# The edges of a feed-forward stage re-ordered: where stores, sums, squares, plain products and the last gains are issued

## The chip, the cores and the metric

One core of one Trainium2 chip runs one encoder layer in float32. The metric is the device time of one execution in microseconds (us), as the median of several runs. Engine names: PE is TensorE, DVE is VectorE, ACT is ScalarE, POOL is GpSimd, SP is SyncE, which issues most DMAs.

## What is computed

512 positions of width 2048 pass through a mixer (state-space and attention heads, not touched here), the output projection `w_out`, a feed-forward stage of width 5632 and an embedding gate:

```python
x = x + concat([y_ssd, y_mla]) @ w_out
h = rms_norm(x, ffn_norm_w)
u = causal_dwconv(h @ w_ffn_up, ffn_conv_w, ffn_conv_b)   # width 3
gate, up = u[..., :D_FF], u[..., D_FF:]
x = x + (silu(gate) * up) @ w_ffn_down
g = sigmoid(rms_norm(x, ple_norm_w) @ w_ple_gate + b_ple_gate)
x = x + g * rms_norm(p @ w_ple_proj, ple_post_norm_w)
return rms_norm(x, final_norm_w)
```

## The kernel before

**Products.** Every float32 operand is split into a high and a low part, and a product takes three matmuls (`acc3`: hi*hi, hi*lo, lo*hi). In the feed-forward both parts are float16: `Scaled.two` has ACT write the high part of a weight unit (`w`, L1040) and DVE the low part (L1041), after a scale `scq` is known for the group of units.

**Units and steps.** A weight unit is 512 x 256 values (512 KB). The up product has 11 chunks `c`, each of four groups `gi` of four units; the down product has groups of two units. `work` lists their order: from chunk 1 on, each up group is followed by a down group of an earlier chunk. One call of `Scaled.step` belongs to one unit: it writes out the parts of the unit two ahead (`split(i + 3)`), the load of the unit nine ahead (`load(i + 10)`, on SP), the look at the unit eight ahead (`look(i + 9)`: ACT takes the sum of absolute values of `raw` into `wst`, L997), POOL's block sums (`sums`), and whatever stands in the tables `first` and `agenda` for this step. Then the unit's matmuls are written out, and in their middle `mid` puts a tiny matmul `tot` (L250) for a group whose looks are complete (`stat`, L266); DVE makes the scale from it (L258 to L260).

**Plain and block units.** A plain unit (`plain_mm`) has 24 matmuls of 512 columns. A block unit (`blocks_mm`, L1242) forms each 2 x 2 block product with seven multiplications, 42 matmuls of 256 columns; it needs POOL's sums of the weight and of the activations, and DVE puts its four PSUM banks together in `blocks_out` (L1264 to L1268), where a plain group has two banks and no such step. In chunk 0 the first `PLAIN` groups are plain. There are seven banks for products. The activations `z` become float16 pairs `x0`, `x1` in `prep_a` (all 512 columns), POOL overwrites `z` with sums in `prep_sums`, `prep_b` makes `x3` and `x2` of them, and `prep_c` overwrites the upper half of `x0`, which plain units read as it was.

**The order of the work.** From the line `feed.enter_context(tc.manual_schedule())` to the end of the feed-forward, each engine's instructions stand in the order in which the code writes them. An engine takes its own queue strictly in order. Ahead of chunk 0 stands a prologue: the embedding projection (`proj.mm`, 16 PSUM banks `pp`, each copied by ACT to `prj` and stored to DRAM as `pnd`), mixed with `prep_a`. The feed-forward's banks are opened when `psum` is closed (`php.close()`).

**Later.** From chunk 1's end on, each of 17 steps runs one entry of `spare`: `proj_square` loads a `prj` tile back into one of three buffers `f` and has ACT sum its squares (L926); `proj_norm` follows. In the last eight down units, `renorm` makes the pair `xg` of each finished `xT[j]` (ACT `xgh`, DVE `xgl`) and adds its square to the sum `n2`, right behind the DVE instruction that finishes `xT[j]` (L1390).

## Time and profile before

| what | value |
|---|---|
| median of 3 runs | 2255.2 us (2254.92 to 2260.88) |
| the profiled execution: its time, its span | 2259.95 us, 2257.9 us |
| mean granted TensorE clock in it | 0.98 |
| PE, DVE, ACT, POOL busy | 96%, 68%, 58%, 43% of the span |

The profile shows one execution; its span runs from the first to the last instruction. PE's busy share is an upper bound: matmuls overlap, and one that runs at half clock counts as busy for twice the time. Slices in which fewer matmuls start than elsewhere are therefore read beside it.

### The profile page before, as it was taken

Reading aid. Unit: us, or ns where it says so; the run is one execution under the profiler, and the core shown is the slowest. Engines: PE = TensorE matmul, PEld = TensorE weight load, DVE = VectorE, ACT = ScalarE, POOL = GpSimd, SP = SyncE. Lnnn points to the kernel's source line nnn. Section 1 sums busy time; section 2 is a strip of 40 time slices with the busy share of each in tenths; the row PEclk is TensorE's granted clock in tenths of the full one; section 3 lists DMA queues with packets and bytes.
Section 4 is the critical chain, followed back from the end, with each engine's and each line's share of the span. In section 5 each row is a group of like instructions: output and inputs, shape, how many; then the busy total and the mean of one; then the engine's idle time right before and its main releaser. Section 6 shows DMA issues by size and latency. Waiting matters only on the chain.

```text
span 2257.9 us, 34811 instructions
## 1 busy us (share of the span) xinstructions
PE 2166.0 (96%) x13476; PEld 1618.2 (72%) x13476; DVE 1536.6 (68%) x2364; ACT 1315.5 (58%) x2031; POOL 961.1 (43%) x949
## 2 busy tenths in 40 slices
PE   9999999999997889879999999999999999999998
PEld 7888887777884377546777777777777777755886
DVE  5597767666437677455778777777777777765545
ACT  4333434433335767566777777777777777755324
POOL 3203320000125465435666566566666666613111
PEclk9999998999998989989999999999999999999999
DMA  7432222322224223333333333333333333333432
GB/s 244 140 99 84 67 60 71 98 71 93 95 92 140 93 94 95 121 102 114 113 113 107 109 103 113 108 109 113 111 114 104 113 112 113 103 102 141 145 108 84
DMA packets 211877, 243.27 MB, mean 108 GB/s; under 512 B 8192, under 2 KB 187520, under 8 KB 211328
## 3 DMA queue, kind: packets, MB, share of 16 engines
q1 hardware_dynamic: 210144, 236.53, 32.9%
q0 software_dynamic: 1280, 4.20, 0.5%
q8 instruction: 105, 1.72, 0.3%
q14 instruction: 60, 0.49, 0.1%
q10 hardware_dynamic: 288, 0.34, 0.0%
HBM read 228.45 MB, written 12.58 MB: 107 GB/s over the span
## 4 chain that ended last, share of the span: by engine, by line
PE 69%; DVE 12%; DMA 7%; ACT 7%; issue 2%; POOL 2%; SPq 0%; ACTq 0%; DVEq 0%; POOLq 0%
PE pu L1242 21%; DVE w L1041 5%; PE pn L160 4%; PE pn L162 4%; PE pn L161 4%; PE pd L160 3%; PE pd L161 3%; PE pd L162 3%; DMA raw<-in_w_ffn_up_dram 3%; PE pw L160 3%; DMA prj<-pnd 3%; PE pw L161 3%; PE pw L162 3%; PE pg L162 2%; PE pg L161 2%
## 5 line engine op out<-in xcount | busy, mean ns | idle before, releaser
L1242 PE MATMUL pu<-x,w 128*128 128x256 f16 x6888 | 767.1, 274 | 14.3 <-DVE e L1264 7.2
L1242 PEld LDWEIGHTS <-w 128*128 128x128 f16 x6888 | 673.2, 98 | 105.6 <-DVE e L1264 7.8
L1041 DVE SCALAR_TENSOR_TENSOR w<-raw,scq,w 128x768 f16<-128x768 f32 (+1 forms) x264 | 339.7, 1287 | 242.6 <-ACT w L1040 240.6
L997 ACT ACTIVATE junk<-raw 128x1024 fp8e4<-128x1024 f32 x264 | 277.6, 1052 | 241.2 <-DMA raw<-in_w_ffn_down_dram 123.3
L1040 ACT ACTIVATE w<-raw,scq 128x768 f16<-128x768 f32 (+1 forms) x264 | 266.1, 1008 | 80.3 <-PE pn L162 47.6
L160 PE MATMUL pn<-h,w 128*128 128x512 f16 x704 | 270.4, 384 | 12.7 <-DVE e L1264 8.7
L162 PE MATMUL pn<-h,w 128*128 128x512 f16 x704 | 270.0, 384 | 4.3 <-DVE w L1041 4.3
L161 PE MATMUL pn<-h,w 128*128 128x512 f16 x704 | 270.4, 384 | 0.0
L1027 POOL TENSOR_TENSOR sum<-raw 128x256 f32<-128x256 f32 x164 | 147.1, 897 | 250.2 <-DVE sct L258 137.8
L137 ACT CAST whi<-raw 128x1024 fp32r<-128x1024 f32 x108 | 113.0, 1049 | 226.4 <-PE pg L162 75.6
L138 DVE TENSOR_TENSOR wlo<-raw,whi 128x1024 fp32r<-128x1024 f32 x108 | 140.6, 1302 | 146.7 <-ACT whi L137 142.1
L1041 DVE SCALAR_TENSOR_TENSOR w<-sum,scq,w 128x1024 f16<-128x1024 f32 x164 | 233.5, 1424 | 5.2 <-ACT w L1040 2.3
L1340 POOL TENSOR_TENSOR o<-o,e 128x510 f32<-128x510 f32 x82 | 114.7, 1409 | 219.9 <-ACT e L1335 219.9
L1040 ACT ACTIVATE w<-sum,scq 128x1024 f16<-128x1024 f32 x164 | 186.1, 1135 | 2.5 <-PE pu L1242 2.1
L160 PEld LDWEIGHTS <-w 128*128 128x128 f16 x800 | 79.0, 99 | 129.6 <-issue 27.4
L1030 POOL TENSOR_TENSOR sum<-raw,sum 128x256 f32<-128x256 f32 x164 | 169.1, 1031 | 0.0
L1029 POOL TENSOR_TENSOR sum<-raw 128x256 f32<-128x256 f32 x164 | 157.0, 957 | 0.0
L162 PEld LDWEIGHTS <-w 128*128 128x128 f16 x800 | 79.2, 99 | 108.5 <-DVE w L1041 8.9
L161 PEld LDWEIGHTS <-w 128*128 128x128 f16 x800 | 79.0, 99 | 98.5 <-issue 16.9
L198 POOL TENSOR_TENSOR n1sq<-n1sq,n1sq 128x512 f32<-128x512 f32 x14 | 20.7, 1480 | 272.7 <-ACT n1sq L192 272.7
L1028 POOL TENSOR_TENSOR sum<-sum,raw 128x256 f32<-128x256 f32 x164 | 129.1, 787 | 12.9
L1390 DVE SCALAR_TENSOR_TENSOR xT<-pn,inv,xT 128x512 f32<-128x512 f32 x176 | 124.3, 744 | 4.3 <-PE pn L162 0.9
(368 smaller groups left out, 3927.1 us busy)
## 6 DMA issues: line engine op xcount, KB each, us to landing
raw<-in_w_ffn_up_dram SPq DMA_DIRECT2D x176, 512.0 KB, 3.5
raw<-in_w_ffn_down_dram SPq DMA_DIRECT2D x88, 512.0 KB, 3.5
raw<-in_w_in_dram SPq DMA_DIRECT2D x40, 512.0 KB, 3.6
raw<-in_w_out_dram SPq DMA_DIRECT2D x32, 512.0 KB, 3.5
raw<-in_w_ple_gate_dram SPq DMA_DIRECT2D x32, 512.0 KB, 3.7
raw<-in_w_in_dram SPq DMA_DIRECT2D x16, 424.0 KB, 3.9
xd<-xt POOLq DMA_DIRECT2D x16, 256.0 KB, 4.5
xT<-xd SPq DMA_DIRECT2D x16, 256.0 KB, 3.8
```

Of the source, the lines that this page charges most:

```text
L138: nc.vector.tensor_tensor(lo, raw, hi.bitcast(F32), ALU.subtract)
L160: nc.tensor.matmul(ps, a[0], b[0], start=first, stop=False)
L161: nc.tensor.matmul(ps, a[0], b[1], start=False, stop=False)
L162: nc.tensor.matmul(ps, a[1], b[0], start=False, stop=last)
L997: nc.scalar.activation(junk, self.raw[i], AF.Abs, accum_out=st[0][:, st[1]:st[1] + 1], saturate=False)
L1027: e(t[:, 0], r[:, :, 0], r[:, :, 2], ALU.add)
L1028: e(t[:, 1], t[:, 0], r[:, :, 1], ALU.subtract)
L1029: e(t[:, 2], r[:, :, 1], r[:, :, 0], ALU.subtract)
L1030: e(t[:, 3], r[:, :, 3], t[:, 1], ALU.subtract)
L1040: nc.scalar.activation(v[0], src, AF.Copy, scale=q)
L1041: nc.vector.scalar_tensor_tensor(v[1], src, q, v[0], ALU.mult, ALU.subtract)
L1242: nc.tensor.matmul(ps, wt[wi], xx[xi], start=st0 and i == 0 and half == 0, stop=sp0 and i == 2, skip_group_check=True)
```

## The change

Six edits, the diff cut to its core:

1. The 16 stores of `pnd` are issued by POOL instead of SP.
2. The looks at units 4 to 8 leave the prologue; those at 4 to 7 stand in step 0 between the last `prep_a`, and `early` passes their `stat` on within step 1.
3. `prep_sums` for all pairs is written in step 2, the last pair first (it was two pairs a step from step 2); `prep_b` moves from steps 5 to 8 to steps 8 to 11, and `prep_c` from steps 11 to 14 to steps 15 to 18.
4. `PLAIN` goes from 3 to 4, so that all of chunk 0 is plain.
5. The `out` of the first block group, (c, gi) = (1, 0), stands in `first`, ahead of the step's weight split.
6. A square's load and its sum stand two steps apart, one pair for each up group from chunk 2 on; `gain_hi` (with the square) and `gain_lo` stand one and two steps behind the unit that finishes `xT[j]`.

```diff
-                nc.sync.dma_start(pnd[t, nb], pr)
+                nc.gpsimd.dma_start(pnd[t, nb], pr)
...
-    def proj_square(t, nb, new):
-        pr = new("prj")
-        nc.sync.dma_start(pr, pnd[t, nb])
-        nc.scalar.activation(junk[:, :512], pr, AF.Square, accum_out=pss[:, t, nb:nb + 1], saturate=False)
+    pload = {}
+    def proj_load(t, nb, new):
+        pload[t, nb] = new("prj")
+        nc.sync.dma_start(pload[t, nb], pnd[t, nb])
+    def proj_square(t, nb):
+        nc.scalar.activation(junk[:, :512], pload[t, nb], AF.Square, accum_out=pss[:, t, nb:nb + 1], saturate=False)
...
-    def renorm(j, gname, nsum):
-        xg[j] = split_gain(xT[j], C(gname, j, j + 1), "xg")
-        nsum.add(xT[j])
+    def gain_hi(j):
+        xg[j] = slot("xgh", F32R), slot("xgl", F32R)
+        nc.scalar.activation(xg[j][0], xT[j], AF.Copy, scale=C("pleg", j, j + 1))
+        n2.add(xT[j])
+    def gain_lo(j):
+        nc.vector.scalar_tensor_tensor(xg[j][1], xT[j], C("pleg", j, j + 1), xg[j][0].bitcast(F32),
+                                       ALU.mult, ALU.subtract)
...
+        def early(self):
+            self.st16old.update(self.st16)
+            self.st16 = {}
...
-            self.look(i + 9)
+            if i:
+                self.look(i + 9)
...
-    PLAIN = 3
+    PLAIN = 4
...
-    fw.look(5)
     for t in range(NT):
         proj.mm(3, t)
-        fw.look(6 + t)
...
-                    for k in (0, 1):
-                        if 2 <= n < 6:
-                            plan(agenda, 1, lambda kp=n * 2 - 4 + k: prep_sums(kp))
-                        if 5 <= n < 9:
-                            plan(agenda, 1, lambda kp=n * 2 - 10 + k: prep_b(kp))
-                        if PLAIN * 4 - 1 <= n < PLAIN * 4 + 3:
-                            plan(agenda, 1, lambda kp=(n - PLAIN * 4 + 1) * 2 + k: prep_c(kp))
-                    if n < 2:
-                        for j in range(8 + n * 4, 12 + n * 4):
+                    if n == 2:
+                        for kp in (7, 0, 1, 2, 3, 4, 5, 6):
+                            plan(agenda, 1, lambda kp=kp: prep_sums(kp))
+                    if n == 0:
+                        for j in range(8, 12):
+                            plan(agenda, 1, lambda j=j: (prep_a(j), fw.look(j - 3)))
+                    if n == 1:
+                        plan(first, 1, fw.early)
+                        for j in range(12, 16):
                             plan(agenda, 1, lambda j=j: prep_a(j))
-                parts, g = ffn_step()
+                    if 8 <= n < 12:
+                        plan(agenda, 1, lambda kp=n * 2 - 16: (prep_b(kp), prep_b(kp + 1)))
+                if 15 <= self.c * 16 + n < 19:
+                    plan(agenda, 1, lambda kp=(self.c * 16 + n - 15) * 2: (prep_c(kp), prep_c(kp + 1)))
+                parts, g = fw.step()
...
-                plan(agenda, k, f)
+                plan(first if f is out and (self.c, gi) == (1, 0) else agenda, k, f)
+            if squares and self.c > 1:
+                t_nb = squares.pop(0)
+                plan(agenda, 2, lambda: proj_load(*t_nb, fslot))
+                plan(agenda, 4, lambda: proj_square(*t_nb))
...
             if up.c == NCK - 1:
-                renorm(j, "pleg", n2)
+                plan(agenda, 1, lambda j=j: gain_hi(j))
+                plan(agenda, 2, lambda j=j: gain_lo(j))
```

On ACT, at the end of the prologue before: `w` is the high part of a weight unit, `junk,wst` a look at `raw`, `prj<-pp` the copy that frees a bank of the projection.

```order
L1040 ACTIVATE w_1263_5860<-raw_5270,scq_5607 128x1024
L997 ACTIVATE junk,wst_5867<-raw_5728 128x1024
L918 COPY prj_5876<-pp_5869 128x512
L997 ACTIVATE junk,wst_5867<-raw_5798 128x1024
L918 COPY prj_5887<-pp_5880 128x512
L997 ACTIVATE junk,wst_5867<-raw_5863 128x1024
L918 COPY prj_5898<-pp_5891 128x512
L997 ACTIVATE junk,wst_5867<-raw_5865 128x1024
L918 COPY prj_5909<-pp_5902 128x512
L1040 ACTIVATE w_1279_5924<-raw_5272,scq_5607 128x1024
```

The same place now:

```order
L1053 ACTIVATE w_1263_5860<-raw_5270,scq_5607 128x1024
L918 COPY prj_5874<-pp_5867 128x512
L918 COPY prj_5884<-pp_5877 128x512
L918 COPY prj_5894<-pp_5887 128x512
L918 COPY prj_5904<-pp_5897 128x512
L1053 ACTIVATE w_1277_5917<-raw_5272,scq_5607 128x1024
L1053 ACTIVATE w_1278_5920<-raw_5274,scq_5607 128x1024
L1166 CAST x_1282_5929<-z_5830 128x512
L1006 ACTIVATE junk,wst_5932<-raw_5728 128x1024
L1166 CAST x_1285_5936<-z_5845 128x512
```

The four looks have moved behind the last four copies and two weight splits.

On ACT, in the stretch of the squares before: `junk,pss<-prj` is one square, in a step that looks at a unit and starts the next unit's parts.

```order
L1040 ACTIVATE w_1557_7983<-raw_7578,scq_7954 128x768
L1040 ACTIVATE w_1558_7986<-sum_7867,scq_7954 128x1024
L997 ACTIVATE junk,wst_7991<-raw_7919 128x1024
L926 ACTIVATE junk,pss<-prj_8005 128x512
L1040 ACTIVATE w_1567_8038<-raw_7648,scq_7954 128x768
L1040 ACTIVATE w_1568_8041<-sum_7922,scq_7954 128x1024
L997 ACTIVATE junk,wst_7991<-raw_7989 128x1024
```

The first square now (`prj_8292` is loaded at the step of the two `o`, two steps above the square):

```order
L1332 ACTIVATE o_8288<-e_8208,cst,taps_8229 128x512
L1332 ACTIVATE o_8290<-e_8208,cst,taps_8229 128x512
L1053 ACTIVATE w_1623_8334<-raw_7926,scq_8183 128x768
L1053 ACTIVATE w_1624_8337<-sum_8224,scq_8183 128x1024
...
L1053 ACTIVATE w_1628_8393<-raw_7985,scq_8183 128x768
L1053 ACTIVATE w_1629_8396<-sum_8283,scq_8183 128x1024
...
L1344 ACTIVATE e_8208<-e_8208,taps_8229 128x512 x2
L930 ACTIVATE junk,pss<-prj_8292 128x512
L1053 ACTIVATE w_1634_8455<-raw_8038,scq_8312 128x1024
```

A square stood in every step, in the step of its load; now it stands once in six steps, two steps behind its load.

On DVE, where the first block group of chunk 1 is put together, before: the two `w` are the low parts for a later unit, `taps` and `e<-pu` are the `out` that frees PSUM banks.

```order
L1041 SCALAR_TENSOR_TENSOR w_1435_7029<-raw_6571,scq_6871,w_1435_7029 128x768
L1041 SCALAR_TENSOR_TENSOR w_1436_7032<-sum_6908,scq_6871,w_1436_7032 128x1024
L1312 TENSOR_SCALAR taps_7042<-cst,scp_6611,cup 128x6
L1264 TENSOR_TENSOR e_7023<-pu_6757,e_7023 128x2x256
L1265 TENSOR_TENSOR e_7023<-pu_6759,e_7023 128x256
```

The same group now:

```order
L1321 TENSOR_SCALAR taps_6920<-cst,scp_6538,cup 128x6
L1275 TENSOR_TENSOR e_6914<-pu_6638,e_6914 128x2x256
L1276 TENSOR_TENSOR e_6914<-pu_6640,e_6914 128x256
L1277 TENSOR_TENSOR e_6914<-pu_6641,e_6914 128x256
L1278 TENSOR_TENSOR e_6914<-e_6914,pu_6639 128x256
L1279 TENSOR_TENSOR e_6914<-pu_6640,e_6914 128x2x256
L1054 SCALAR_TENSOR_TENSOR w_1425_6927<-raw_6511,scq_6758,w_1425_6927 128x768
```

The five instructions that empty the banks have moved ahead of the weight split.

## Rows read from the trace of the kernel before

**Rows 1.** Windows: length; busy (instructions) of PE, PEld, DVE, ACT, POOL; clock; DMA.

```profile
697.60:710.60 13.00, 0.12 (x1) 0.10 (x1) 5.50 (x6) 6.50 (x14) 6.41 (x6) 0.61 0.49 161
710.60:857.40 146.80, 128.80 (x800) 81.09 (x800) 100.15 (x136) 93.41 (x147) 79.07 (x82) 0.93 0.29 92
...
937.00:1049.00 112.00, 84.25 (x550) 53.84 (x548) 53.46 (x91) 68.27 (x117) 45.60 (x55) 0.91 0.32 106
```

**Rows 2.** PE's timeline (start, us, what): two neighbouring plain units' first matmuls.

```profile
772.46 0.38 PE L160 MATMUL pu<-x,w 128*128 128x512 f16 x1
...
777.64 0.38 PE L160 MATMUL pu<-x,w 128*128 128x512 f16 x1
```

**Rows 3.** The chain that ended last, from 822 us: start, us, what.

```profile
821.97 9.19 PE pu L1242 x84
...
833.77 3.77 DVE w L1041 x2
...
838.69 0.60 DVE e L1264
```

**Rows 4.** ACT's timeline from 706 us; in brackets idle time and what ended it.

```profile
706.76 1.06 ACT L997 ACTIVATE junk<-raw 128x1024 fp8e4<-128x1024 f32 x1 [5.95 <-DMA raw<-in_w_ffn_up_dram]
...
710.46 2.19 ACT L1040 ACTIVATE w<-raw,scq 128x1024 f16<-128x1024 f32 x2
...
718.56 1.64 ACT L1153 CAST x<-z 128x512 f16<-128x512 f32 x3
```

**Rows 5.** SP's timeline at the prologue's end.

```profile
692.67 4.41 SPq L919 DMA_DIRECT2D pnd<-prj  x4
702.97 0.93 SPq L985 DMA_DIRECT2D raw<-in_w_ffn_up_dram  x2
```

**Rows 6.** DVE's timeline in the prologue.

```profile
681.96 2.07 DVE L1158 SCALAR_TENSOR_TENSOR z<-xT,gs,n1rb 128x512 f32<-128x512 f32 x3
...
696.66 1.22 DVE L1158 SCALAR_TENSOR_TENSOR z<-xT,gs,n1rb 128x512 f32<-128x512 f32 x1
```

**Rows 7.** POOL's timeline beside the second of these.

```profile
697.41 1.06 POOL L1171 TENSOR_TENSOR z<-z,z 128x256 f32<-128x256 f32 x1
```

**Rows 8.** PE's waits from 710.7 to 857.4 us: total, times, longest.

```profile
PE pu L1242 <- DVE e L1264: 7.2, 2, 3.9
PE pu L1242 <- ACT x L1153: 3.4, 1, 3.4
...
PE tot L250 <- DVE st L266: 2.2, 1, 2.2
PE pu L1242 <- DVE x L1154: 1.9, 2, 1.3
```

**Rows 9.** Groups by line, 937 to 1049 us: busy, mean ns, idle before, releasers.

```profile
L1242 PE MATMUL pu<-x,w 128*128 128x256 f16 x399 | 44.7, 273 | 1.9 <-DVE w L1041 1.9
L160 PE MATMUL pn<-h,w 128*128 128x512 f16 x48 | 21.2, 441 | 12.6 <-DVE e L1264 8.7 <-ACT w L1040 3.9
```

**Rows 10.** The tile `prj`: the squares (ns), who waits for it, its transfers.

```profile
L926 ACT ACTIVATE junk<-prj x16: 629/630/631, 922.8 to 1032.5; 128x512 fp8e4<-128x512 f32 x16
...
  ACT junk L926: 48.5, 16
...
DMA to landing us min/median/max: 2.0/3.8/5.6
```

**Rows 11.** DVE's timeline: two neighbouring weight splits of the last down units.

```profile
2048.99 1.42 DVE L1041 SCALAR_TENSOR_TENSOR w<-raw,scq,w 128x1024 f16<-128x1024 f32 x1 [0.81 <-ACT w L1040]
...
2055.94 1.43 DVE L1041 SCALAR_TENSOR_TENSOR w<-raw,scq,w 128x1024 f16<-128x1024 f32 x1 [0.81 <-ACT w L1040]
```

**Rows 12.** PE's waits, 2003 to 2062.5 us, then 2062.5 to 2100 us.

```profile
PE pn L162 <- DVE w L1041: 0.9, 1, 0.9
...
PE pg L161 <- DVE wlo L138: 0.6, 1, 0.6
```

**Rows 13.** The tile `xd`: stores that POOL issues at the kernel's start (ns).

```profile
L326 POOL DMA_DIRECT2D xd<-xt x16: 547/557/747, 7.5 to 76.5; - x16
```

More of the change, by code (lines that the diff above doesn't have):

```diff
@@ L1059, in step @@
             i = self.done
-            self.st16old.update(self.st16)
-            self.st16 = {}
+            self.early()
             self.stat()
@@ L1268, in blocks_out @@
         tt(e[:, 1:4:2], halves(q[2]), e[:, 1:4:2], ALU.add)
-    spare = []
-    def ffn_step():
-        got = fw.step()
-        if spare:
-            spare.pop(0)()
-        return got
+    squares = [(t, nb) for t in range(NT) for nb in range(4)]
     class Up:
@@ L1360, in group @@
             for k, f in zip(w, (out, conv0, conv1, conv2, conv3, done)):
-                plan(agenda, k, f)
+                plan(first if f is out and (self.c, gi) == (1, 0) else agenda, k, f)
[3 more added lines that the diff above has]
+                plan(agenda, 4, lambda: proj_square(*t_nb))
+                if not squares:
+                    plan(agenda, 4, proj_norm)
             if gi == 3:
@@ L1376, in ffn_down @@
     def ffn_down(up, cu, inv):
-        w, g = ffn_step()
+        w, g = fw.step()
         w = w.rearrange("p s (k c) -> p s k c", c=256)
@@ L1400, in block_kernel @@
             ups[c].group(i)
-            if c == 1 and i == 3:
-                spare.extend(lambda t=t, nb=nb: proj_square(t, nb, fslot) for t in range(NT) for nb in range(4))
-                spare.append(proj_norm)
         else:
@@ L1408, in block_kernel @@
             ffn_down(ups[c], 2 * i + 1, inv)
+    for k in sorted(agenda):
+        for f in agenda.pop(k):
+            f()
     D("x2", xT[5])
```

## The prediction

> **What bounds the kernel now.** I read the page's busy shares first (PE 96%, the others 43 to 68%), so time is won only where PE stands still or runs at half clock. The windows by stage show where that is [rows 1]: nothing runs on PE in the 13.0 us from 697.6, 800 matmuls start in the next 146.8 us, and 550 in the 112.0 us from 937. The clock column gives 0.93 and 0.91 for the last two, so part of each ran at the lower of the two levels (1.2 instead of 2.4 GHz), behind the stalls. To turn counts into lost time I need a unit's undisturbed length. A plain unit (24 matmuls of 512 columns) takes 777.64 - 772.46 = 5.18 us [rows 2], a down unit is the same 24 matmuls, and two block units (84 matmuls) take 9.19, so 4.59 each [rows 3]. Everything below is in these lengths. The steps of the feed-forward outside the stages named here, and all of the mixer, the change leaves as they are.
>
> **Stage A, the end of the prologue (13.0 us).** PE can't open the feed-forward's banks before ACT has copied the last `prj`. It does so just before 710.46, where it goes on to `w`, behind looks at units whose weights arrive late: ACT sat idle for 5.95 us before the look at 706.76 [rows 4]. The loads were late because SP issues them in order, behind four stores that wait for ACT's copies, and behind a raw buffer that DVE frees: they go out at 702.97 [rows 5]. DVE was late since POOL's sums ran beside it: the same `z` instruction takes 0.69 us alone (2.07 for three) and 1.22 with POOL at work [rows 6, 7].
> The change takes all three away. The four looks stand behind the copies, the stores leave SP, and POOL's sums wait for the last `z` pair, thus for the last `prep_a`. What is left between PE's last projection matmul and its first `pu` is one copy of 0.57 us and the hand-over, about 0.9, so `pu` starts at 698.5. **Gain 12.1.**
>
> **Stage B, chunk 0 up to the first down unit (146.8 us).** Before, it holds twelve plain and eight + four block units: 12 x 5.18 + 12 x 4.59 = 117.2. So 29.6 are lost. In the changed kernel it is 16 x 5.18 + 8 x 4.59 = 119.6; the fourth plain group costs 2.4. What remains to be estimated is how much of the 29.6 comes back, wait by wait [rows 8]:
> - The half clock behind the 13 us gap goes with the gap, and so do the early waits for a slow `prep_a`: at 0.69 us, eight DVE instructions a step are 5.5 us, about one unit, and a unit's `x` is wanted two steps later.
> - `out` of a block group, 7.2 us in two waits. Block groups take four of seven banks, so the next block group waits for `out` before its fourth bank. One of the two waits stood between chunk 0's last group and chunk 1; that group is now plain and takes two banks (2 + 4 are under 7), so it is gone. In the other DVE first did two `w` (3.77 us) and then `e` in 0.60 [rows 3]; now `out` is ahead of them. I leave 0.5 for it.
> - Block units wait for `prep_c` (3.4 and 1.9). The 3.4 came from a late ACT, the 1.9 from DVE, which has two `w` and four taps in its queue ahead of `prep_c`. This order moves to the new border unchanged, so I keep the 1.9 and 1.0 for ACT.
> - New: the looks at units 4 to 7 stand in step 0, and `tot` of that group is in the middle of unit 1. ACT does two `w` (2.19), four casts (3 in 1.64) and four looks (1.06, about 1.15 with the read of the sum) behind its last copy: 2.2 + 2.2 + 4.6 = 9.0 us, while PE is there after 5.18 + 2.6 = 7.8 [rows 2, 4]. PE waits 1.2.
> - `prep_b` now meets the taps of group 1 in step 9 as it met those of group 0 in step 5; the scale then came late and led to the 2.2 us wait at `tot`. ACT starts that step on time now; I leave 0.9.
>
> Together 0.5 + 2.9 + 1.2 + 0.9 = 5.5 of waits, so 125.1 instead of 146.8. **Gain 21.7**, with 0 and 20 as bounds for the waits.
>
> **Stage C, the squares (112.0 us).** 399 matmuls of block units are 9.5 units, 43.6 us; 3 x 48 of down units are 6 units, 31.1 [rows 9]. So 37.3 are lost. ACT waits 48.5 us in 16 times for `prj` [rows 10], each time in the step that issued the load; weight parts behind it come late, and through DVE the banks too. Now the load is two steps ahead, at least 9.2 us, and the slowest transfer of a `prj` took 5.6. The load also needs one of three `f` buffers: an odd group holds two from step +1 until POOL's product at +4, a square one from +1 to +3, so the next load, six steps on, finds one free. The square itself, 0.63 us on ACT, comes once in six steps, 4 x 4.59 + 2 x 5.18 = 28.7 us, and ACT is busy 58% of the span; the weight parts are made two units ahead, which covers it. If that cover were gone, 16 x 0.63 = 10 us would come back. On SP the load stands behind the step's weight load and ahead of the next step's, which is wanted a step later. **Gain 37.3.**
>
> **Stage D, the last down units.** DVE needs 6.95 us from one weight split to the next [rows 11], PE 5.18, since `xT`, `xgh`, `xgl` go to and fro between DVE and ACT. PE lives on its lead of two units and waits only at the end, 0.9 and 0.6 [rows 12]. A step behind, DVE has about 1.4 + 4 x 0.75 = 4.4 us without waiting. What is left over behind the last unit are the pairs of the last `xT`, which the gate wants only at the end of its first pass. The pipelined ends hide part of such a wait, so I take **2.0**, between 0 and 4.
>
> **The sum.** 12.1 + 21.7 + 37.3 + 2.0 = 73.1 off the profiled execution, 2259.95, is 2186.9. That execution was 4.75 us above the median; off 2255.2 it is 2182.1, and I predict **2182**.
>
> **Stores on POOL.** A store takes POOL 0.56 us, at most 0.75, at a place where DVE works beside it [rows 13]; 16 are 9 us, spread over the whole prologue, and POOL's sums start only when the last `z` is read. On POOL's queue the prologue's `rt` stands behind two of them, which follow copies that are done before `rt`'s input is. I take nothing for it. The Trainium skill, page "SBUF — State Buffer", section "SBUF: two separate sides", warns of the contrary: a DMA issued by POOL can't write its descriptors while DVE holds the port that the two share, and takes about 3.1 us instead of 0.62 beside a DVE copy. By that figure, as an estimate, 16 stores would hold POOL for some 50 us instead of 9, and the sum would be 2 to 4 us longer. No row of this case shows such a store; how a late POOL would act here is the second rival.
>
> **The rivals.**
> 1. *The stalls move with the border* from plain to block units. For it: the same instructions stand in the same order around it, and ACT and DVE have little slack there. Against: the bank wait has a cause that is gone. If PE loses before the first block units what `L1242` lost there before, 7.2 + 3.4 + 1.9 = 12.5 and a stretch at half clock of 2 to 3 us, in place of my 3.4: 2182 + 11 = **2193**.
> 2. *POOL's queue is late.* POOL's 32 sums at 1.06 us [rows 7] are 34 us. They can start at about 714: step 1 ends at 698.5 + 2 x 5.18 + 1.2 = 710, and ACT's last casts follow. So they end at 748, and the last pair is wanted in step 11, at 698.5 + 1.2 + 11 x 5.18 = 757. A POOL that comes to them 13 us later costs 4: **2186**. For that the 16 stores must end at 727, 28 us behind the last copy at 698.5, each some 1.8 us longer than the 0.56 of [rows 13]; against it stands 0.75 at most.
> 3. *The squares' loads still come late*, because SP issues them behind a weight load that waits for its buffer. Then stage C keeps its loss: **2219**. Against: the wait was for landings, not for issue, and two steps of room are new.
> 4. *Slower.* SP is one queue. If a `prj` load has to wait for its `f` buffer, all weight loads behind it wait too, 16 times. The buffer comes free with POOL's product, the last link of a chain over DVE, ACT and POOL. Against it: it has three steps to spare, by the count in stage C. To eat up 73.1 us, PE must lose 73.1 / 16 = 4.6 at each load, beyond the two units (9 us) that are made ahead; from a hold of about 14 us each it is slower, **2256** and more.
>
> **How the numbers follow.** My forecast has 0.70; its own range is 2172 to 2190, from all waits of stage B gone (-5.5), stage D at 4 (-2) and some scatter, to 8 us more of waits. Rival 1 has 0.15, rival 2 0.06, rival 3 0.05, rival 4 0.02, something else between 2190 and 2250 0.02. A range from 2171 to 2204 holds forecast and rivals 1 and 2, with the 6 us by which executions of the kernel before differ. What a measurement here can tell from no change is 0.3%, 6.8 us: faster than 2248 in all but rival 4, so faster 0.97, same 0.01, slower 0.02.
>
> **What would show it.** A: `pu` starts within 2 us of the last projection matmul and the clock stays at 1.00. B: unit 24 starts about 126 us later; PE waits for `st` once early by 1 us; no wait of `L1242` for `e` over 1 us; DVE's `z` at 0.69 throughout. C: no ACT wait for `prj`, 28.7 us for each group of six units throughout. D: PE in step through the last eight units. It would be wrong if the border shows waits over 10 us, if ACT still waits for `prj`, or if SP shows holds before `prj` loads.

## The result and the profile after

The changed kernel takes 2196.19 us (median, 2194.23 to 2197.52) where the kernel before took 2255.06: a ratio of 0.9734 (95% interval 0.9715 to 0.9754), 58.9 us less. The forecast was 73 us less. The profiled execution took 2197.52 us, with a span of 2195.8.

The page, busy shares and clock: PE has risen from 96 to 98%, and the clock line has no slice below 9.

```profile
PE 2150.7 (98%) x13404; PEld 1608.5 (73%) x13404; DVE 1521.5 (69%) x2357; ACT 1308.0 (60%) x2024; POOL 960.9 (44%) x947
PEclk9999999999999999999999999999999999999999
```

I cut both traces at the same units of work: first `pu`, first down unit (24), unit 56 (behind the squares of before), unit 252 (the last of chunk 10's up groups is done), the gate, the end. Windows of the kernel before (columns as in [rows 1]):

```profile
710.61:857.44 146.83, 128.84 (x800) 81.12 (x800) 100.19 (x136) 93.44 (x147) 79.07 (x82) 0.93 0.29 92
857.44:1049.09 191.65, 163.90 (x1142) 111.41 (x1140) 112.97 (x182) 124.78 (x203) 90.91 (x103) 0.95 0.33 108
1049.09:1992.90 943.81, 939.36 (x7156) 694.30 (x7154) 716.75 (x1082) 693.64 (x1013) 604.03 (x610) 1.00 0.35 111
1992.90:2062.49 69.59, 64.62 (x294) 28.40 (x291) 44.86 (x75) 38.03 (x58) 18.23 (x15) 0.98 0.32 114
2062.49:2257.90 195.41, 183.67 (x840) 151.47 (x840) 103.98 (x123) 73.35 (x115) 31.70 (x22) 0.98 0.34 113
```

The same five of the kernel after:

```profile
696.80:826.84 130.04, 122.74 (x728) 71.27 (x728) 91.07 (x129) 91.29 (x147) 76.55 (x81) 0.99 0.35 111
826.84:982.51 155.67, 154.52 (x1140) 110.57 (x1140) 117.12 (x182) 118.19 (x177) 99.24 (x102) 1.00 0.35 111
982.51:1932.11 949.60, 939.88 (x7156) 694.29 (x7154) 710.43 (x1083) 699.42 (x1038) 603.19 (x611) 1.00 0.36 114
1932.11:2001.66 69.55, 65.18 (x294) 28.96 (x292) 52.82 (x80) 41.13 (x63) 25.38 (x16) 0.95 0.35 122
2001.66:2195.80 194.14, 183.43 (x842) 151.68 (x840) 99.90 (x117) 69.94 (x110) 29.71 (x20) 0.98 0.33 111
```

The reader should read the second column of each, and then the clock. Against the forecast:

| | before | after | gained | forecast |
|---|---|---|---|---|
| A: to the first `pu` | 710.61 | 696.80 | 13.8 | 12.1 |
| B: to unit 24 | 146.83 | 130.04 | 16.8 | 21.7 |
| C: to unit 56 | 191.65 | 155.67 | 36.0 | 37.3 |
| the chunks between | 943.81 | 949.60 | -5.8 | 0 |
| D: last down units | 69.59 | 69.55 | 0.0 | 2.0, with the gate |
| the gate | 195.41 | 194.14 | 1.3 | |
| span | 2257.9 | 2195.8 | 62.1 | 73.1 |

**A.** Of the 13 us in which PE stood still [rows 1] 0.7 are left (waits of PE from 682 to 697.5 us; total, times, longest). That is 12.2 of the 13.8 in the table; of the rest, 1.0 lies ahead of the projection, whose first matmul starts at 670.76 instead of 671.76, in the part that the change leaves alone, and 0.6 inside it.

```profile
PE pu L160 <- ACT prj L918: 0.7, 1, 0.7
```

The tile `prj` (ns, first and last start) shows the stores, which take POOL what [rows 13] had said, and that nobody on ACT waits for the squares' loads any more:

```profile
L919 POOL DMA_DIRECT2D pnd<-prj x16: 539/539/631, 673.2 to 697.0; - x16
...
who waited for it (us, times):
  POOL pnd L919: 15.1, 15
  DVE ms L934: 2.0, 1
...
```

The transfers of the loads are as long as before. [Rows 10] has loads and stores in one line; for the loads alone the changed kernel's trace has 3.7, 3.9 and 4.8 us (minimum, median, maximum), that of the kernel before 3.7, 3.8 and 5.1.

**B.** PE's waits from 697.5 to 826.84 us, the counterpart of [rows 8]:

```profile
PE pu L1253 <- ACT x L1166: 3.1, 2, 2.6
PE pu L1253 <- DVE x L1167: 2.5, 4, 1.5
PE tot L250 <- DVE st L266: 0.8, 1, 0.8
PE pu L1253 <- DVE e L1275: 0.2, 1, 0.2
```

The 7.2 us for `e` have become 0.2, but the block units still wait for `x`, 5.6 us where they had waited 5.3.

**The chunks between.** All waits of PE there are for `tot`, the total that a scale is made from, at the turn from one chunk to the next. Before they came to 4.4 us in four waits (`PE tot L250 <- DVE sct L258: 4.4, 4, 1.3`); after, to 9.8 in eight (982 to 1932 us):

```profile
PE tot L250 <- DVE sct L258: 7.2, 7, 1.8
PE tot L250 <- DVE st L266: 2.6, 1, 2.6
```

### The profile page after: what moved, and what is told of

Same layout as the page of the kernel before. It is cut to its first block, busy times and chain, and to the rows that moved or that the text cites. A ratio compares the mean times of both kernels' runs of the same rounds, so it can differ in the third digit from the quotient of the medians.

```text
span 2195.8 us, 34633 instructions
## 1 busy us (share of the span) xinstructions
PE 2150.7 (98%) x13404; PEld 1608.5 (73%) x13404; DVE 1521.5 (69%) x2357; ACT 1308.0 (60%) x2024; POOL 960.9 (44%) x947
## 4 chain that ended last, share of the span: by engine, by line
PE 45%; DVE 24%; ACT 13%; DMA 11%; issue 4%; POOL 2%; SPq 0%; ACTq 0%; DVEq 0%; POOLq 0%
DVE w L1054 12%; DMA raw<-in_w_ffn_up_dram 6%; DMA raw<-in_w_ffn_down_dram 5%; ACT w L1053 4%; ACT junk L1006 3%; PE pd L160 3%; PE pu L1253 3%; PE pd L162 3%; PE pd L161 3%; PE pw L160 3%; DVE xT L1405 3%; PE pw L161 3%; PE pw L162 3%; PE pg L162 3%; PE pg L161 3%
## 5 line engine op out<-in xcount | busy, mean ns | idle before, releaser
L1253 PE MATMUL pu<-x,w 128*128 128x256 f16 x6720 | 743.6, 273 | 5.8 <-ACT x L1166 3.1
L1253 PEld LDWEIGHTS <-w 128*128 128x128 f16 x6720 | 654.9, 98 | 91.8 <-issue 7.0
L1054 DVE SCALAR_TENSOR_TENSOR w<-raw,scq,w 128x768 f16<-128x768 f32 (+1 forms) x264 | 335.2, 1270 | 195.1 <-ACT w L1053 194.1
L137 ACT CAST whi<-raw 128x1024 fp32r<-128x1024 f32 x108 | 113.2, 1049 | 238.8 <-PE pg L162 84.5
L1040 POOL TENSOR_TENSOR sum<-raw 128x256 f32<-128x256 f32 x160 | 142.0, 888 | 227.4 <-DVE sct L258 131.5
L1053 ACT ACTIVATE w<-sum,scq 128x1024 f16<-128x1024 f32 x160 | 181.5, 1134 | 0.0
L160 PEld LDWEIGHTS <-w 128*128 128x128 f16 x832 | 81.5, 98 | 112.5 <-issue 20.5
L162 PEld LDWEIGHTS <-w 128*128 128x128 f16 x832 | 81.5, 98 | 99.7 <-issue 2.1
L1042 POOL TENSOR_TENSOR sum<-raw 128x256 f32<-128x256 f32 x160 | 151.2, 945 | 0.0
L161 PEld LDWEIGHTS <-w 128*128 128x128 f16 x832 | 81.5, 98 | 89.7 <-issue 2.8
```

Source lines behind the costliest of these rows:

```text
L160: nc.tensor.matmul(ps, a[0], b[0], start=first, stop=False)
L161: nc.tensor.matmul(ps, a[0], b[1], start=False, stop=False)
L162: nc.tensor.matmul(ps, a[1], b[0], start=False, stop=last)
L1040: e(t[:, 0], r[:, :, 0], r[:, :, 2], ALU.add)
L1042: e(t[:, 2], r[:, :, 1], r[:, :, 0], ALU.subtract)
L1053: nc.scalar.activation(v[0], src, AF.Copy, scale=q)
```

## The experiments

Twelve runs in three series, each series on a chip of its own; each edit is made on the changed kernel (run 10 is that kernel itself). The kernel before took 2256.36 us beside the first four, 2263.86 beside the next four and 2265.86 beside the last, so ratios to the kernel before are compared across series, and times only inside one. The changed kernel's own ratio came to 0.9734 and, in run 10, to 0.972, so a ratio between 0.970 and 0.976 decides little, and the stage that an edit touches is read in the trace. Profiled executions of one program differ too: where the prologue is the changed kernel's own, the first `pu` starts anywhere from 692.47 to 698.62 us. PE's wait just before it is 0.67 us in every one of these traces, and the projection ahead of it already starts at 666.41 to 672.56; so the edits didn't make this difference, and one to the prologue is read from the wait. Chunk 0 and its border repeat far better: stage B takes 130.04 and 130.08 us in two executions of the changed kernel, and 129.78 to 130.52 in the experiments that leave it alone (1, 4, 11, 12).

**1. The norm of the projection two steps later.** `proj_norm` is the reduction behind the last square, on DVE, and a power on POOL.

```diff
-                    plan(agenda, 4, proj_norm)
+                    plan(agenda, 6, proj_norm)
```

> The changed kernel with one edit: proj_norm two steps behind the last square instead of in its step. Theory: in the last square's step DVE stands in front of proj_norm until ACT has done the square (DVE ms waited 2.0 us there), and PE pays for it at two scales (2.7 and 1.9 us at 1380 and 1388); with the edit those two waits shrink to about 1 in total, 2196.2 - 3.5 = 2192.7. Rival: the waits come from ACT's squares themselves, and the place of proj_norm is no matter: 2196 within 1.5, and the waits near 1380 us stay above 3 in sum.

Measured: 2190.36 us (2187.97 to 2193.28), ratio 0.9702 (0.9686 to 0.9718), more than the theory gave. In its trace the chunk with the norm takes 116.57 us, in the changed kernel 119.68. Windows, the changed kernel first:

```profile
1331.28:1450.96 119.68, 115.35 (x874) 84.74 (x873) 86.71 (x134) 85.09 (x128) 74.19 (x77) 1.00 0.35 111
```

and with the norm later:

```profile
1329.32:1445.89 116.57, 115.19 (x874) 84.69 (x873) 87.89 (x134) 86.22 (x128) 77.51 (x77) 1.00 0.36 114
```

The mechanism stands in the changed kernel's timelines of DVE, POOL and ACT (start, us, idle time and what ended it):

```profile
1371.87 0.17 DVE L934 TENSOR_REDUCE ms<-pss 128x4 f32<-128x16 f32 x1 [1.96 <-ACT junk L930]
...
1372.32 1.04 POOL L936 TENSOR_TENSOR prs<-ms,cst 128x4 f32<-128x4 f32 x1 [13.22 <-DVE st L266]
1373.34 1.43 POOL L1040 TENSOR_TENSOR sum<-raw 128x256 f32<-128x256 f32 x1
...
1381.45 1.26 POOL L1351 TENSOR_TENSOR o<-o,o 128x512 f32<-128x512 f32 x1
...
1382.74 0.63 ACT L1360 ACTIVATE junk<-o 128x512 fp8e4<-128x512 f32 x1 [1.66 <-POOL o L1351]
...
1383.49 0.16 DVE L266 TENSOR_REDUCE st<-gst 128x1 bf16<-128x4 f32 x1 [4.44 <-ACT junk L1360]
```

Read from the top: DVE's reduction stands in the step of the last square and waits 1.96 us for it. POOL's power waits for DVE, and POOL's whole queue waits with it, 13.22 us; the `sum` and the chunk's last products follow late, ACT's `abs` waits for them, the maximum `st` for ACT, and PE stands 2.6 us at `tot`. With the norm later POOL starts the same `sum` 30.9 us into the chunk instead of 42.1:

```profile
1360.18 0.73 POOL L1040 TENSOR_TENSOR sum<-raw 128x256 f32<-128x256 f32 x1 [3.68 <-DVE sct L258]
```

PE's two waits for `tot` there, 2.56 and 1.77 us, become one of 1.38. In the nine other traces with the squares spread out and the norm where the change put it this chunk takes 118.15 to 120.23 us, in run 9, with the norm later again, 117.39. So the norm costs 2 to 3 us. The rest of the 5.8 us between the two medians can't be put down to it: the other chunks and the unit that waits for the final total are shorter too in this execution, and these move from run to run.

**2. `prep_c` one step earlier**, in steps 14 to 17.

```diff
-                if 15 <= self.c * 16 + n < 19:
-                    plan(agenda, 1, lambda kp=(self.c * 16 + n - 15) * 2: (prep_c(kp), prep_c(kp + 1)))
+                if 14 <= self.c * 16 + n < 18:
+                    plan(agenda, 1, lambda kp=(self.c * 16 + n - 14) * 2: (prep_c(kp), prep_c(kp + 1)))
```

> The changed kernel with one edit: each prep_c one step earlier (steps 14 to 17). Theory: at the border from plain to block units PE waits because prep_c stands in the step just ahead of the unit that reads it, behind that step's weight split, look and taps; one step of room takes most of the four waits of units 16 to 19 (8.1 us over their lengths): 2196.2 - 6.5 = 2189.7, unit 16 under 6 us. Rival: ACT and DVE are late as such at the border (prep_b, the scale behind the taps), so a queue place one step up only makes the weight parts late instead: 2196 within 2, with PE waiting for w in place of x.

Measured: 2192.19 us (2191.44 to 2195.19), ratio 0.9712 (0.9698 to 0.9727), between the two. The trace decides against the theory: units 16 and 17 run clean (4.59 and 4.61 us), but unit 20 takes 12.21 us, and stage B 131.75 instead of 130.04. PE waits at the new place:

```profile
PE pu L1253 <- DVE e L1275: 4.5, 1, 4.5
```

What the median gained lies elsewhere in the trace (a first `pu` at 694.40, shorter waits at the chunks), where executions of one program scatter.

**3. Chunk 0 with three plain groups**, as before, with `prep_c` in steps 11 to 14 again.

```diff
-    PLAIN = 4
+    PLAIN = 3
...
-                if 15 <= self.c * 16 + n < 19:
-                    plan(agenda, 1, lambda kp=(self.c * 16 + n - 15) * 2: (prep_c(kp), prep_c(kp + 1)))
+                if 11 <= self.c * 16 + n < 15:
+                    plan(agenda, 1, lambda kp=(self.c * 16 + n - 11) * 2: (prep_c(kp), prep_c(kp + 1)))
```

> The changed kernel with PLAIN back at 3 (and prep_c at steps 11 to 14, as before), all else as changed. Theory: the fourth plain group costs 2.4 us of PE and saves the wait of the next block group for a bank (about 5.9 us with its half clock): without it 2196.2 - 2.4 + 5.9 = 2199.7, a wait of L1253 for e of over 3 us at unit 16, and the waits for prep_c now at units 12 to 15, where prep_b stands in the same steps, thus up to 5 more. Rival: the bank wait would be gone anyway, since ACT and DVE are on time now: 2193.8.

Measured: 2200.17 us (2199.03 to 2205.96), ratio 0.975 (0.9733 to 0.9767). Stage B takes 138.30 us, 8.3 more than in the changed kernel; PE's waits there:

```profile
PE pu L1253 <- ACT x L1166: 7.2, 1, 7.2
PE pu L1253 <- DVE e L1275: 3.3, 1, 3.3
```

The second bank wait is back, as the theory had it: unit 16 takes 9.54 us instead of a block unit's 4.59, about 5 us, more than the 2.4 that a plain group costs. But the larger part of the 8.3 is another one: the 7.2 us stand in unit 12 (18.41 us), where `prep_c` now follows right on the steps of `prep_b`. The edit moves both, so the 8.3 are not the price of the bank alone.

**4. The squares as before**, load and sum in one step, a square in each of the 16 steps behind chunk 1.

```diff
-            if squares and self.c > 1:
-                t_nb = squares.pop(0)
-                plan(agenda, 2, lambda: proj_load(*t_nb, fslot))
-                plan(agenda, 4, lambda: proj_square(*t_nb))
-                if not squares:
-                    plan(agenda, 4, proj_norm)
+            if squares and (self.c, gi) == (1, 3):
+                for k in range(1, 17):
+                    plan(agenda, k, lambda t_nb=squares.pop(0): (proj_load(*t_nb, fslot), proj_square(*t_nb)))
+                plan(agenda, 17, proj_norm)
```

> The changed kernel with the squares as they were: load and square in the same step, in 16 steps on end from the end of chunk 1, all else as changed. Theory: the stretch loses again what it lost before, 36 us, and the later chunks get back what their scales wait for the squares (up to 6): 2196.2 + 36 - 0 to 6 = 2226 to 2232. Rival: part of the gain of this stretch came from the earlier edits, which left ACT and DVE less late when the squares begin: under 2220.

Measured: 2237.89 us (2234.11 to 2239.39), ratio 0.9907 (0.989 to 0.9924): 41.7 us more, beyond the theory's range. Stage C takes 203.05 instead of 155.67 us; the tile `prj` shows why:

```profile
  DMA prj<-pnd: 55.6, 16
```

ACT waits 55.6 us for 16 landings, 7.1 more than before [rows 10], 3.5 us a piece, where a load's landing has a median of 3.7. The order is not quite that of before: from the eighth square on it stands ahead of the step's other work on ACT, where before it stood behind it. The first seven waits come to 22.1 us (22.7 before), the other nine to 33.5 (25.8 before), so this is where the 7.1 come from. The squares are the largest part of the change. The edit undoes two things at once, the load two steps ahead and the spread over six units; what each is worth alone is not shown. The chunks between come to 943.5 us, as before the change, and as with the norm later (944.1). That would put down what they lose in the changed kernel to the norm and not to the spread squares, but in run 9, with the norm later as well, they come to 951.84, so it is not shown.

**5. The taps of the plain groups one step later**, so that DVE makes the next weights' scale first.

```diff
-            w = ((1, 1, 2, 2, 2, 2) if final else (1, 1, 2, 3, 3, 4) if plain else
+            w = ((1, 1, 2, 2, 2, 2) if final else (1, 1, 3, 4, 4, 5) if plain else
```

> The changed kernel (2196.2) with the taps of the plain groups (and what follows them) one step later, so that DVE reaches the scale of the next weight group first. In the changed kernel ACT waits 2.70 us (at 776.5) and 4.86 us (at 799.9) for that scale while DVE does four taps in 2.97 us. Theory (the border loses because ACT and DVE wait for one another in a bad order): both waits shrink by about 3 us each, units 16 to 19 lose about 4 instead of 8.1 us, 2192. Rival (the border has too much work on ACT and DVE whatever its order, as the run with prep_c a step earlier suggests, where the stall went to unit 20): the four taps now hold up the subtractions of x, 2196 within 2.

Measured: 2194.31 us (2191.89 to 2197.34), ratio 0.9699 (0.9684 to 0.9713). Stage B takes 127.62 instead of 130.04 us, a gain of 2.4, but only 1.1 of it at the theory's place: unit 16 takes 5.26 instead of 9.45 us, and units 17 and 19 in return 7.00 and 8.50 instead of 5.11 and 5.61. Units 20 to 23 give most of the rest.

**6. POOL's sums in the order of before**, pair 0 first, two pairs a step.

```diff
-                    if n == 2:
-                        for kp in (7, 0, 1, 2, 3, 4, 5, 6):
-                            plan(agenda, 1, lambda kp=kp: prep_sums(kp))
+                    if 2 <= n < 6:
+                        for k in (0, 1):
+                            plan(agenda, 1, lambda kp=n * 2 - 4 + k: prep_sums(kp))
```

> The changed kernel with POOL's sums in the order of before, pair 0 first and two pairs a step, so that they need not wait for the last z. The chunk's prologue then has POOL at work beside DVE's z and x. Theory (it is the sums that stretched z from 0.69 to 1.22 us): the 16 z and subtractions in steps 0 and 1 take up to 8 us longer, unit 1 waits for its total and unit 3 for x, 3 to 6 us with the half clock behind: 2199 to 2203. Rival (DVE has slack there, since it waits for ACT): 2196 within 2.

Measured: 2201.1 us (2195.72 to 2208.84), ratio 0.9731 (0.9706 to 0.9756). The ratio is no other than the changed kernel's, and the times scatter too far; the trace decides. Unit 1 takes 12.35 instead of 6.13 us, and DVE's `z` and `x` are at 1.21 us each from the moment that POOL starts (one shown, then PE's wait and the matmul behind it):

```profile
701.75 1.21 DVE L1171 SCALAR_TENSOR_TENSOR z<-xT,gs,n1rb 128x512 f32<-128x512 f32 x1
...
711.02 0.16 PE L250 MATMUL tot<-st,onesb 128*128 128x1 bf16 x1 [5.56 <-DVE st L266]
711.04 0.59 PE L160 MATMUL pu<-x,w 128*128 128x512 f16 x1
```

In the changed kernel they take 0.74 and 0.69 us (one shown), so the theory holds: waiting with the sums for the last `z` is worth 6.2 us, and a part of that is the clock, since the matmul behind the wait takes 0.59 instead of 0.38 us.

```profile
701.50 0.74 DVE L1171 SCALAR_TENSOR_TENSOR z<-xT,gs,n1rb 128x512 f32<-128x512 f32 x1
```

The first `pu` is not late here: PE's wait before it stays at 0.67 us. The Trainium skill, page "SBUF — State Buffer", section "SBUF: two separate sides", describes it: a vector operation with two SBUF inputs and a POOL operation that reads SBUF share a port pair, and whichever comes first holds it for its whole instruction. The trace agrees: DVE's starts are 1.13 us apart here and 0.60 to 0.67 in the changed kernel.

**7. The looks between the last copies again**, none in step 0.

```diff
+    fw.look(5)
     for t in range(NT):
         proj.mm(3, t)
+        fw.look(6 + t)
...
-                            plan(agenda, 1, lambda j=j: (prep_a(j), fw.look(j - 3)))
+                            plan(agenda, 1, lambda j=j: prep_a(j))
```

> The changed kernel with the looks at units 4 to 8 between the last copies of the projection again, and none in step 0. Theory (the 5.95 us of idle ACT before was the late load, which stores on POOL cure by themselves): five looks of 1.25 us make the last copy some 3 us late, the 0.93 us wait for the total in unit 1 goes, together 2197 to 2199. Rival (the looks alone made stage A, their weights are still late): pu starts 8 us or more later, 2204 and above.

Measured: 2199.96 us (2197.34 to 2200.86), ratio 0.9722 (0.9705 to 0.9738). The first `pu` starts at 701.62 us, outside what the other executions show, behind a wait of 5.99 instead of 0.67 us; unit 0 takes 6.58 instead of 5.18, unit 1 in return 5.21 instead of 6.13. PE's first `pu`, and ACT, where a load is still late:

```profile
701.62 0.58 PE L160 MATMUL pu<-x,w 128*128 128x512 f16 x1 [5.99 <-ACT prj L918]
...
698.43 1.06 ACT L1006 ACTIVATE junk<-raw 128x1024 fp8e4<-128x1024 f32 x1 [3.24 <-DMA raw<-in_w_ffn_up_dram]
```

So the looks at their old place cost 5.3 + 1.4 - 0.9 = 5.8 us of stage A and chunk 0; the time, with its ratio of 0.9722, doesn't decide. The outcome lies between theory and rival: of the 5.95 us of idle ACT [rows 4] 3.24 are left with the stores on POOL.

**8. `out` of the first block group behind the weight split again.**

```diff
-                plan(first if f is out and (self.c, gi) == (1, 0) else agenda, k, f)
+                plan(agenda, k, f)
```

> The changed kernel with out of chunk 1's first group behind the step's weight split again. Theory: unit 20 waits for the bank as before, 10 us instead of 4.9 with the half clock behind it, and the weights that come earlier save nothing: 2201. Rival (the work at the border is conserved, so that the weight split that is now earlier shortens units 21 to 24): 2196 within 2.

Measured: 2200.09 us (2198.62 to 2201.79), ratio 0.9724 (0.971 to 0.9739). Unit 20 takes 11.29 instead of 4.93 us, stage B 135.65, and PE waits as before:

```profile
PE pu L1253 <- DVE e L1275: 4.1, 1, 4.1
```

In its stage the theory holds, and units 23 and 24 give 1.5 us of it back; the ratio, as it is, can't tell the two kernels apart.

**9. Three edits together:** the norm later (1), `prep_c` earlier (2), the taps later (5).

> The changed kernel with three edits together: the norm of the projection two steps later, prep_c one step earlier (steps 14 to 17), the taps of the plain groups one step later. Theory (order at the border, and a norm that meets the chunk's total): with prep_c early the units 16 to 19 run without waits, and with the scale ahead of the taps ACT is not late for the out of unit 20, which was the price of prep_c early alone (12.2 us for that unit); stage B 122 to 124 instead of 130.0 us, the chunk with the norm 116.6 instead of 119.7: 9 to 11 us less than the changed kernel run beside it. Rival (the work at the border is conserved): only the norm's 3 to 6 us.

Measured: 2196.44 us (2195.68 to 2198.93), ratio 0.9691 (0.9678 to 0.9704); the changed kernel beside it (10) 2204.61. It is 8.2 us faster, and the fastest ratio of all. But not by the theory's way: the chunk with the norm takes 117.39 instead of 120.07, and stage B only 128.05. Units 16 to 19 are clean, and unit 20 takes 11.89 us. PE there, then DVE:

```profile
805.21 11.32 PE L1253 MATMUL pu<-x,w 128*128 128x256 f16 x87 [4.06 <-DVE e L1275]
```

```profile
797.32 2.96 DVE L1326 SCALAR_TENSOR_TENSOR o<-pu,taps,o 128x511 f32<-128x511 f32 x4
800.20 1.01 DVE L1054 SCALAR_TENSOR_TENSOR w<-raw,scq,w 128x768 f16<-128x768 f32 x1
801.13 2.29 DVE L1054 SCALAR_TENSOR_TENSOR w<-sum,scq,w 128x1024 f16<-128x1024 f32 x1
...
803.65 0.92 DVE L1321 TENSOR_SCALAR taps<-cst,scp,cup 128x6 f32<-128x6 f32 x1
804.48 0.68 DVE L1275 TENSOR_TENSOR e<-pu,e 128x512 f32<-128x512 f32 x1
```

DVE goes without a pause through four taps and a weight split, and comes to `out` when PE has long been there: PE arrives earlier and waits for the same queue. In the changed kernel DVE (third of the busy times) is at work for 21.9 of the 26.4 us that units 16 to 19 take, where 18.4 had been counted for PE:

```profile
780.80:807.21 26.41, 20.80 (x172) 17.17 (x171) 21.91 (x28) 18.72 (x32) 19.79 (x21) 0.94 0.28 90
```

That, with (2) and (5), points to too little DVE time in these steps; another order of the same work moves the stall by one to four units, and takes away 2.4 us of it at most.

**10. The changed kernel once more.**

> The changed kernel once more, beside the three edits, since the kernel before was 7.5 us slower in the job of the last four runs than in the others. Its ratio to the kernel before should be 0.9734 again, within 0.002; the start of the first pu and the waits for tot at the chunks show how far two profiled executions of one kernel differ.

Measured: 2204.61 us (2199.93 to 2205.98), ratio 0.972 (0.9705 to 0.9734). B and C repeat (130.08 and 156.41), the chunks take 955.66 where the first execution had 949.60; the difference is in the waits at the chunks' ends, one of which follows a look on ACT that waited 5.21 us for a weight to land.

**11. The stores on SP again.**

```diff
-                nc.gpsimd.dma_start(pnd[t, nb], pr)
+                nc.sync.dma_start(pnd[t, nb], pr)
```

> The changed kernel with the stores on SP again. SP then holds each store until its copy is done, and the weight loads behind it. Theory (the stores did their part by holding the loads): looks in step 0 come late, as the look before that waited 5.95 us, and unit 1 waits for its total 3 to 5 us instead of 0.93: 4 to 7 us more than the changed kernel. Rival (it was the raw buffer that DVE freed late): within 2 us of the changed kernel.

Measured: 2200.47 us (2197.79 to 2208.66), ratio 0.9713 (0.9692 to 0.9733), 4.1 less than the changed kernel beside it, with overlapping intervals: no loss, though by the median more than the rival's 2 us on the other side. PE's wait before the first `pu` is 0.67 us and unit 1 takes 6.13, as in the changed kernel, so the theory falls, and with looks and sums where they are now the stores' queue doesn't matter.

**12. The gains at once**, `gain_hi` and `gain_lo` behind each `xT` as before.

```diff
-                plan(agenda, 1, lambda j=j: gain_hi(j))
-                plan(agenda, 2, lambda j=j: gain_lo(j))
+                gain_hi(j)
+                gain_lo(j)
```

> The changed kernel with gain_hi and gain_lo issued at once behind each xT, as before. Theory (the stall of stage D): the last two units take 5.5 and 6.5 us again instead of 5.18 and 4.99, 2 us more. Rival (the gate takes back what the units give): no difference in the sum of the last units and the gate.

Measured: 2203.9 us (2201.68 to 2209.59), ratio 0.9726 (0.9709 to 0.9743), no difference in time to the changed kernel beside it. In the trace the last two units take 5.63 and 6.53 us instead of 5.18 and 4.99, 2.0 more, and the gate 196.22 instead of 194.06, 2.2 more. PE's waits from 1952 to 2100 us are back ([rows 12]); in the changed kernel there is none in this window:

```profile
...
PE pxt L1447 <- ACT xk L1449: 1.2, 1, 1.2
PE pn L162 <- DVE w L1054: 0.9, 1, 0.9
PE pg L161 <- DVE wlo L138: 0.8, 1, 0.8
...
```

(The line left out at the top is the wait for the final total, which in this trace falls inside the window.) The theory holds for this stage, and the gate adds to it. That the time doesn't show these 4 us is within what the chunks scatter by (951.84 to 958.86 in the four traces of this series).

## Why the prediction was right, and where its sum was not

The forecast was 2182, in a range from 2171 to 2204; the time, 2196.19, lies in that range, but outside the forecast's own, 2172 to 2190, and near rival 1 (2193). The wide range holds it because it was drawn to take in rival 1. The forecast counted 73.1 us of gain; the span shows 62.1. The missing 11.0 are +1.7 in A, -4.9 in B, -1.3 in C, -0.7 in D with the gate, and -5.8 in the chunks.

- **A was right in sum and partly wrong in its cause.** PE's wait went from 12.88 to 0.67 us, 12.2 for the 12.1 forecast; the 1.7 that the table has on top are luck, since they come from ahead of the wait. The prediction named three things: looks, stores, and sums beside `z`. With looks and sums where they are now, the stores' queue makes no difference (11). The looks alone bring 5.3 of the 12.2 back (7). The sums, with the stores on POOL, are worth 6 us, but in unit 1 of stage B and not in this wait (6). Sums and stores both at their old places were not tried together, and there one edit may have done part of the other's work: in (6) POOL's sums start behind its last store, at 698.32, while in the kernel before, with the stores on SP, they started at 684.77, beside the prologue's own `z`. So what made the other 7 us of the wait is not shown.
- **B: the term of `prep_c` was mis-sized.** The failed step is "This order moves to the new border unchanged, so I keep the 1.9 and 1.0 for ACT". Measured are 2.5 for DVE and 3.1 for ACT, with part of unit 16 at half clock: units 16 to 19 take 26.4 us (780.80 to 807.21) where 4 x 4.59 = 18.4 were counted, 8.0 lost against 2.9. The prediction put the old 3.4 down to "a late ACT" and cut it to 1.0 without a reason why ACT should be on time at the new border. ACT is late because DVE makes its next scale behind four taps, before the change as well as after it, and with the taps behind the scale (5) unit 16 takes 5.26 instead of 9.45 us. ACT's wait before the change, at the old border:

```profile
778.53 0.94 ACT L1040 ACTIVATE w<-raw,scq 128x768 f16<-128x768 f32 x1 [3.58 <-DVE scq L260]
```

  ACT's and DVE's timelines of the changed kernel at the new one:

```profile
776.47 0.94 ACT L1053 ACTIVATE w<-raw,scq 128x768 f16<-128x768 f32 x1 [2.70 <-DVE scq L260]
...
773.10 2.97 DVE L1326 SCALAR_TENSOR_TENSOR o<-pu,taps,o 128x511 f32<-128x511 f32 x4
```

  So rival 1's mechanism acted, in the `x` half of its price (5.3 us of waits, and a stretch at half clock) and not in the `e` half: the bank wait is gone, both for the plain group (3) and for `out` (8). In runs 2, 5 and 9 another order of the work at the border is worth 2.4 us at most.
- The rest of B held in sum, 2.4 us lost for 0.5 + 1.2 + 0.9 = 2.6: `tot` in unit 1 waits 0.8 for 1.2 forecast, and unit 1 takes 6.13, 0.95 more than 5.18. Not in each term: the 0.9 for `prep_b` did not come, and 0.7 is a wait of the first down unit for `h`, which the forecast did not have.
- **C was right**: 36.0 for 37.3; 155.67 us are 20 x 4.59 + 12 x 5.18 = 154.0 and 1.7 of waits. Putting the squares back (4) cost 47.4 in the stage, 11 more than the change had won there, with ACT's waits 7.1 longer in an order that is not quite that of before. That the loads' landings were what ACT waited for is shown; how much of the gain is the earlier load and how much the spreading is not. One reading was off without harm: the 5.6 us for the slowest transfer of a `prj` is that of a store, the slowest load took 5.1.
- **D was right in kind:** 2.0 in the last units by (12), and 2 more in the gate. In the profile before against after it is hidden, since the unit that waits for the final total took 12.22 instead of 10.41 us. That unit takes 8.62 to 13.38 in the traces of this study, without a pattern that follows an edit; what sets it stays open.
- **"The steps of the feed-forward outside the stages named here ... the change leaves as they are" was wrong.** The squares and the norm were moved into the later chunks, and I costed the squares' ACT time there (0.63 us in 28.7) and not the norm's place in POOL's queue. That is worth 2 to 3 us, shown by (1) and (9). The remaining 3 of the 5.8 stay open; they are less than the 6.1 by which two executions of the changed kernel differ.
- Rival 2 (POOL late through its stores) fell: 0.54 us a store, and POOL's sums of `z` end at 742, with no wait for them in the trace. The 3.1 us that the Trainium skill, page "SBUF — State Buffer", section "SBUF: two separate sides", gives for a DMA of POOL's beside a vector copy don't show here: nine of the 16 stores ran beside DVE's `z` and `x`, at 0.54 us each, and the longest, 0.63, while DVE was idle. But none of these DVE instructions is a copy, so the page's own case did not arise. Rivals 3 and 4 fell with the counterpart of [rows 10]: no wait of ACT for `prj`, and in SP's queue from 895 to 1420 us only loads of weights wait.

## What to carry to other kernels

When a stall is to vanish because the work around it moves, ask whether the engine that makes the wanted tile has the time for it in those steps; if it has not, a new order carries the stall to the next consumer, as it did at the border three times. Price each moved instruction on the queue where it lands, one of 1 us too: a small reduction whose input is made in the same step held POOL for the products behind it. And where executions of one program differ by 6 us, read an edit of 2 us from the stage that it touches, in several traces, and not from the time.

## What the runs showed of the hardware

- DVE's and POOL's operations on SBUF slow each other: DVE's `z` and `x` of 512 fp32 columns from 0.74 and 0.69 to 1.21 us, POOL's 256 columns from 0.73 to 1.06 [rows 7]. A store's issue on POOL beside the same DVE instructions took 0.54 us, no more than the 16 at the kernel's start [rows 13].
- A short wait can cost PE its clock. Behind 4.37 us at `tot` the next matmuls take 0.63 instead of 0.38 us, and lie 0.43 apart; that is the lower of the two levels (1.2 GHz). The unit lost 12.22 - 5.18 = 7.0 us, 2.7 more than the wait:

```profile
1949.62 0.16 PE L250 MATMUL tot<-st,onesb 128*128 128x1 bf16 x1 [4.37 <-DVE st L266]
1949.64 0.59 PE L160 MATMUL pn<-h,w 128*128 128x512 f16 x1
1950.03 0.63 PE L161 MATMUL pn<-h,w 128*128 128x512 f16 x1
```

  Behind 2.56 us at 1383.71 in the same trace they stay at 0.38. But behind 2.63 us in unit 16, one matmul and another 0.49, matmuls of 256 columns take 0.42 instead of 0.27, and the window from there (columns as in [rows 1]) has a granted clock of 0.54:

```profile
784.58:788.00 3.42, 2.93 (x14) 2.02 (x14) 3.42 (x5) 3.17 (x5) 3.34 (x4) 0.54 0.02 5
```
- The kernel before took medians of 2255.06 to 2265.86 us in the four series, 0.5% apart, more than most of these edits were worth.
